# State product and decay transposes moved by one step each in a Mamba-2 branch beside large products

## The chip, the cores and the metric

The kernel runs on one core of one Trainium2 chip. The metric is the device time of one execution in microseconds (us). A core has TensorE (PE in the profile; PEld is its weight load), VectorE (DVE), ScalarE (ACT), GpSimd (POOL) and SyncE (SP, which here only issues transfers). PE writes its results to PSUM, in banks of 128 partitions by 512 32-bit numbers; DVE and ACT read them from there.

## The reference, cut to what matters

One decoder layer on 512 positions of width 1024: a norm, one large projection into all branches, three branches in parallel (dilated attention, causal pooling, Mamba-2 SSD), gates, a projection back, and a gated feed-forward with a convolution. The change lies in the SSD branch:

```python
def ssd_scan(x, dt, A, Bm, Cm):
    ...
    a = (dt * A).reshape(b, c, l, h).transpose(0, 3, 1, 2)
    a_cs = jnp.cumsum(a, axis=-1)
    ...
    Lmat = jnp.exp(jnp.where(causal, seg, -jnp.inf)).reshape(b, g, e, c, l, l)
    cb = jnp.einsum("bclgn,bcsgn->bcgls", Cc, Bc)
    y_diag = jnp.einsum("bcgls,bgecls,bcsgep->bclgep", cb, Lmat, xc)
    decay = jnp.exp(a_cs[..., -1:] - a_cs).reshape(b, g, e, c, l)
    states = jnp.einsum("bclgn,bgecl,bclgep->bcgepn", Bc, decay, xc)
    chunk_decay = jnp.exp(a_cs[..., -1]).reshape(b, g, e, c)

    def step(carry, inp):
        st, dec = inp
        return carry * dec[..., None, None] + st, carry
    ...
    out_decay = jnp.exp(a_cs).reshape(b, g, e, c, l)
    y_off = jnp.einsum("bclgn,bcgepn,bgecl->bclgep", Cc, prev, out_decay)
    return (y_diag + y_off).reshape(b, s, h, p)
```

There are 4 chunks of 128 positions and 2 groups of 8 heads. For each pair (chunk c, group gi): `y_diag` is a product with decays inside the chunk, `states` is what the chunk adds to the state, and `y_off` is what the state left by the chunks before contributes.

## The kernel before, in words

**The large products.** All weight products run in 32-bit numbers split into a high and a low part: three products (`mm3`, line 228, matmuls at line 234) replace one. Weights pass through a fixed pipeline: SP loads a block `raw` (line 183), ACT makes the high part `wh` (line 195), DVE the remainder `wl` (line 215), PE multiplies. A job is one such block; a 512-column result with 8 row blocks of weights takes 24 matmuls.

**Steps.** The smaller work of the branches stands between these products. Each such piece is a Python generator: `step()` (line 156), called after a result of the large products (in some jobs twice in one), takes the next waiting item into the running set and lets every running item advance to its next `yield`. A plain `yield` ends the item's part of this step. `yield ROWS`, `yield WHOLE` and `yield REST` postpone what follows to a later phase of the same step: first all items run up to such a mark, then all with `ROWS`, then `WHOLE`, then `REST`. So an item's place among the steps, and its phase, decide where its instructions stand in the queue of each engine. PE, ACT, DVE and POOL run in exactly the order written (line 106, `ORDERED`), each strictly in its queue's order; the semaphores between them are added by the framework from who reads and writes what.

**Buffers.** PSUM has 8 banks: 4 for the large products (`MM`) and 4 (`SM`, line 114) shared by all small pieces: score products `ps`, score transposes `pt`, value products `po`, and those of the SSD branch. A new small tile gets the bank that was given back first, and its first product waits for the last reader of the tile that held the bank. The 512-wide tiles in SBUF come from a common set of 54 (`T`, line 108) in the same way.

**The cumulated decays** (`ssd_prep`, line 834) run between the products of the pooling branch's output, beside the first group of attention heads. One step forms the cumulated decays as `pcs` (lines 873 and 874) and copies them to `acs`; the next step transposes them into `pact` (line 888). DVE copies `pact` (line 890), ACT takes its exponential (line 893), and SP stores both to DRAM (`ad`, line 892; `ed`, line 895). They are read back by transfers much later, in the scan (lines 920 and 926).

**The scan** (`ssd_start`, line 989) begins after the products of the branch's inputs and runs beside the third group of attention heads and the first gates. It puts one `ssd_item` for each (c, gi) on the waiting list in the order `SSD_ORDER` = (0,0), (1,0), (0,1), (2,0), (1,1), (3,0), (2,1), (3,1), with a free place after each; the attention's items take these free places. So a new item starts every second step, and an item takes five steps:

1. the loads of the decays (SP, lines 920 and 926), then in `WHOLE` the transposes of x (`pxs`, line 931), the product `pcb` (line 937), their readers on DVE (lines 933 and 939), and POOL's product with decays `xd` (line 942, not for c = 3)
2. the decays inside the chunk, DVE (line 948) and ACT (line 949)
3. their product with `pcb` on DVE (line 953)
4. for c of 1 and 2: POOL's product of the old state with the chunk's decay, into the new state `nw` (tile `st`, line 957)
5. `py` (line 963), and in `WHOLE`: for c > 0 the product `pyo` with the old state (line 970), DVE's product and sum with it (lines 972 and 973), the addition to the output (line 976); then, for c < 3, the state product `pst` (line 981), which is copied by ACT for c = 0 (line 984) and added to `nw` by DVE otherwise (line 986)

`prev[gi]` holds the group's last state. The next item of the same group reads it in its own steps 4 and 5.

Of the kernel before, what the change touches and what calls it, by code (L numbers as in the profile page):

```python
# [13 lines left out]
OP = mybir.AluOpType  # L14
AX = mybir.AxisListType

P = 128
# [66 lines left out]
def trunk(ctx: ExitStack, tc, out, x, rel_bias, ln1_g, w_in, b_gate, w_a, pool_w, pool_scale, w_b,  # L84
# [3 lines left out]
    act, dve, pool, pe, sp = nc.scalar, nc.vector, nc.gpsimd, nc.tensor, nc.sync  # L88
# [19 lines left out]
    def T(name, dt=F32, shape=(P, S)):  # L108
        return big.tile(list(shape), dt, name=name, tag="t")
# [4 lines left out]
    def SM(name):  # L114
        return psum.tile([P, S], F32, name=name, tag="sm")
# [32 lines left out]
    ROWS, WHOLE, REST = 1, 2, 3  # L148
# [664 lines left out]
    XS, YT, Y = {}, {}, {}  # L813
# [20 lines left out]
    def ssd_prep():  # L834

        f = lambda nme: cst.setdefault(nme, cpool.tile([P, n16], F32, name=nme))
        b16 = cpool.tile([P, 2, SH], F32, name="b16")
        for i, src in enumerate((ssd_dt_bias, ssd_a_log)):
            sp.dma_start(b16[:, i, :], src[0].partition_broadcast(P))

        dr, gr = T("dr"), T("gr")
        sp.dma_start(dr[:8, S - 2:], ssd_d[0].rearrange("(c h) -> c h", h=2))
        sp.dma_start(gr[:8, :P], ssd_norm_w[0].rearrange("(c p) -> c p", p=P))
        yield
        dve.tensor_copy(dr[:8, :P].rearrange("p (h d) -> p h d", h=2),
                        dr[:8, S - 2:].unsqueeze(2).to_broadcast([8, 2, DH]))
        dgc = cst["dgc"] = cpool.tile([P, 16], F32, name="dgc")
        v4 = lambda t: t.rearrange("p (a b) -> p a b", a=4)
        bc = lambda i: b16[:, i, :].unsqueeze(1).to_broadcast([P, 4, SH])
        xx, t, u, s, zz, dtv, a = (f(nme) for nme in ("dtx", "dtt", "dtu", "dts", "dtz", "dtv", "dta"))  # L850
        dve.tensor_tensor(v4(xx), dtr, bc(0), OP.add)
        dve.scalar_tensor_tensor(t, xx, -1.0, xx, OP.mult, OP.max)
        act.activation(t, t, AF.Exp, scale=-1.0)
        act.activation(b16[:, 1, :], b16[:, 1, :], AF.Exp)
        yield
        dve.tensor_scalar(u, t, 2.0, None, OP.add)
        dve.reciprocal(u, u)
        dve.tensor_mul(s, t, u)
        dve.tensor_mul(zz, s, s)
        dve.tensor_scalar(u, zz, 2.0 / 17, 2.0 / 15, OP.mult, OP.add)  # L860
        for d in (13, 11, 9, 7, 5, 3, 1):
            if d == 9:
                yield
            dve.tensor_mul(u, u, zz)
            dve.tensor_scalar(u, u, 2.0 / d, None, OP.add)
        dve.tensor_mul(u, u, s)
        dve.scalar_tensor_tensor(dtv, xx, 0.0, u, OP.max, OP.add)
        dve.scalar_tensor_tensor(v4(a), v4(dtv), -1.0, bc(1), OP.mult, OP.mult)
        yield
        yield  # L870
        yield WHOLE
        ps = SM("pcs")
        pe.matmul(ps[:, :n16], tri, a, start=True, stop=True)
        pe.matmul(ps[:, n16:2 * n16], ones, a, start=True, stop=True)
        for i, r in enumerate((dr, gr)):
            pe.transpose(ps[:, 2 * n16 + 8 * i:2 * n16 + 8 * i + 8], r[:8, :P], eye[:8, :8])
        dve.tensor_copy(dgc, ps[:, 2 * n16:2 * n16 + 16])
        acs, tot, dec = (f(nme) for nme in ("acs", "tot", "dec"))
        dve.tensor_copy(acs, ps[:, :n16])
        dve.tensor_copy(tot, ps[:, n16:2 * n16])  # L880
        dve.tensor_tensor(dec, tot, acs, OP.subtract)
        act.activation(dec, dec, AF.Exp)
        act.activation(tot, tot, AF.Exp)
        yield
        yield WHOLE
        pt = SM("pact")
        for c in range(4):
            pe.transpose(pt[:SH, c * P:(c + 1) * P], acs[:, c * SH:(c + 1) * SH], eye)
        at, et = T("acst"), T("east")
        dve.tensor_copy(at[:SH], pt[:SH])  # L890
        ad = cst["ad"] = dram.tile([SH, S], F32, name="ad")
        sp.dma_start(ad, at[:SH])
        act.activation(et[:SH], pt[:SH], AF.Exp)
        ed = cst["ed"] = dram.tile([SH, S], F32, name="ed")
        sp.dma_start(ed, et[:SH])

    def hb(t, c, h0, n=8):
        return t[:, c * SH + h0:c * SH + h0 + n].unsqueeze(2).to_broadcast([P, n, DH])

    def h3(t):  # L900
        return t.rearrange("p (h d) -> p h d", h=8)

    btok, prev, done = {}, {}, set()
# [9 lines left out]
    def ssd_item(c, gi):  # L913
        cs = slice(c * P, (c + 1) * P)
        dtv, acs, dec, tot, ad, ed = (cst[n] for n in ("dtv", "acs", "dec", "tot", "ad", "ed"))
        als = []
        for q in range(2):
            al = T("al")
            h0 = 8 * gi + 4 * q
            sp.dma_start(al.rearrange("p (h l) -> p h l", h=4), ad[h0:h0 + 4, cs].partition_broadcast(P))  # L920
            als.append(al)
        if c:
            ea = T("ea")
            for i in range(2):
                h0 = 8 * gi + i
                sp.dma_start(ea[DH * i:DH * i + DH].rearrange("p (j l) -> p j l", j=4),
                             ed[h0:h0 + 8 - i:2, cs].partition_broadcast(DH))
        yield WHOLE
        ps = SM("pxs")
        for j in range(4):  # L930
            pe.transpose(ps[:, j * P:(j + 1) * P], XS[4 * gi + j][:, cs], eye)
        xc = T("xc")
        dve.tensor_tensor(h3(xc), h3(ps), hb(dtv, c, 8 * gi), OP.mult)  # L933

        y = Y[gi][:, :, cs]
        pcb = SM("pcb")
        pe.matmul(pcb[:, :P], XS[8 + gi][:, cs], XS[10 + gi][:, cs], start=True, stop=True)
        cbt = T("cbt", F32, (P, P))
        dve.tensor_tensor(cbt, pcb[:, :P], tri, OP.mult)
        if c < 3:  # L940
            xd = T("xd")
            pool.tensor_tensor(h3(xd), h3(xc), hb(dec, c, 8 * gi), OP.mult)  # L942
        yield
        for q in range(2):
            a3 = als[q].rearrange("p (h l) -> p h l", h=4)
            for j in range(4):
                i = c * SH + 8 * gi + 4 * q + j
                dve.tensor_scalar(a3[:, j, :], a3[:, j, :], acs[:, i:i + 1], 0.0, OP.subtract, OP.min)
            act.activation(als[q], als[q], AF.Exp)
        yield  # L950
        for q in range(2):
            a3 = als[q].rearrange("p (h l) -> p h l", h=4)
            dve.tensor_tensor(a3, a3, cbt.unsqueeze(1).to_broadcast([P, 4, P]), OP.mult)
        yield
        if c and c < 3:
            nw = T("st")
            pool.tensor_tensor(h3(nw), h3(prev[gi]), hb(tot, c, 8 * gi), OP.mult)
        yield
        py = SM("py")
        for j in range(4):  # L960
            for i in range(2):
                o, lo = (2 * j + i) * DH, (2 * j + i) % 4 * P
                pe.matmul(py[DH * i:DH * i + DH, j * P:(j + 1) * P], xc[:, o:o + DH],  # L963
                          als[j // 2][:, lo:lo + P], start=True, stop=True)
        by_j = lambda t: t.rearrange("p (j l) -> p j l", j=4)
        yield WHOLE
        if c:
            po = SM("pyo")
            for j in range(4):
                pe.matmul(po[:, j * P:(j + 1) * P], prev[gi][:, j * P:(j + 1) * P], XS[10 + gi][:, cs],  # L970
                          start=True, stop=True)
            dve.tensor_tensor(ea, po, ea, OP.mult)
            dve.tensor_tensor(ea, ea, py, OP.add)
        for j in range(4):
            m = 4 * gi + j
            dve.scalar_tensor_tensor(y[:, j, :], y[:, j, :], cst["dgc"][:, m:m + 1],
                                     by_j(ea if c else py)[:, j, :], OP.mult, OP.add)
        done.add((c, gi))
        if c < 3:
            pst = SM("pst")  # L980
            pe.matmul(pst, btok[gi][:, cs], xd, start=True, stop=True)  # L981
            if c == 0:
                nw = T("st")
                act.copy(nw, pst)
            else:
                dve.tensor_tensor(nw, nw, pst, OP.add)
            prev[gi] = nw

    def ssd_start():
        for m in (8, 9, 0, 1, 2, 3, 10, 4, 5, 6, 7, 11):  # L990
# [366 lines left out]
    def program():  # L1357
# [4 lines left out]
        yield from pool_out_job()  # L1362
        yield Call(lambda: attend(0))
        yield Call(lambda: waiting.insert(3, ssd_prep()))
        for i, job in enumerate(branch_jobs(1, w_b, YB, 8, more=range(7))):
            if i == 3:
# [262 lines left out]
```

## Time and profile before

| what | value |
|---|---|
| three runs | 1044.83, 1042.64, 1044.0 us; median 1044.0 |
| the profiled execution | 1044.41 us, of which the span of the profile is 1042.1 |
| clock granted to PE in it, mean | 0.997 |
| instructions in the span | 13072 |
| state products `pst` (line 981) | 6, in two rows each, from 398.6 to 484.6 us of the span |
| transposes `pact` (line 888) | 4, at 163.5 us |

A row of the profile names the line, the engine, the operation and the tiles as out<-in. Matmuls overlap with those behind them and their ends are modelled, so distances from start to start tell more than durations. A product of plain 32-bit numbers shows as two rows. The idle time in square brackets counts from the modelled end of the engine's instruction before, and the arrow names what ended it.

### The profile page before, as it was taken

To read this page: it belongs to the slowest core of one execution; us is meant where nothing else is said; L and a number is where in the kernel's file an instruction comes from. 1 tells how busy PE (TensorE), PEld (TensorE's weight loads), DVE (VectorE), ACT (ScalarE), POOL (GpSimd) and SP (SyncE) were. 2 spreads that over 40 slices of the span, in tenths; PEclk is the share of its full clock that TensorE was granted. 3 is DMA by queue.
4 is the path that set the end of the run, shared out by engine and by line. 5 is a ranking of instruction groups with operands and counts; after the bars stand their busy time and mean duration, and the time that the engine had idled before them with its cause. 6 is when DMAs were issued, how large, how long until landed. Compare 5 with 4: busy or idle time off the path is not lost.

```text
span 1042.1 us, 13072 instructions
## 1 busy us (share of the span) xinstructions
PE 1028.6 (99%) x5196; PEld 859.2 (82%) x5196; DVE 688.9 (66%) x924; ACT 483.2 (46%) x779; POOL 136.9 (13%) x118
## 2 busy tenths in 40 slices
PE   8999999999999999999999999999999999999997
PEld 8988877898888887777888888898888888888885
DVE  4563556774356658666568755767778769876776
ACT  5432445443474363466555333544445544454332
POOL 1680000000000001100134500001111000111002
PEclk9999999999999999999999999999999999999999
DMA  8445222126322354542244535543222232412222
GB/s 272 128 109 155 88 75 75 31 56 186 102 81 81 81 151 112 142 130 53 81 139 136 181 102 202 165 142 121 82 94 69 81 122 84 159 41 81 81 81 81
DMA packets 116427, 115.51 MB, mean 111 GB/s; under 512 B 5235, under 2 KB 101302, under 8 KB 116367
## 3 DMA queue, kind: packets, MB, share of 16 engines
q1 hardware_dynamic: 115775, 113.83, 36.0%
q8 instruction: 41, 0.67, 0.3%
q10 hardware_dynamic: 592, 0.86, 0.2%
q14 instruction: 19, 0.16, 0.0%
HBM read 110.87 MB, written 2.22 MB: 109 GB/s over the span
## 4 chain that ended last, share of the span: by engine, by line
PE 96%; ACT 1%; DVE 1%; DMA 1%; issue 0%; ACTq 0%; DVEq 0%
PE pa L234 35%; PE pu L234 22%; PE pb L234 12%; PE pqk L234 9%; PE pd L234 7%; PE pa L1480 2%; PE pu L1290 1%; PE ps L661 1%; PE pt L690 1%; PE ppw L234 1%; PE po L702 1%; PE py L963 1%; DMA eye<-in_c_eye_dram 1%; PE uT L1497 1%; PE pyo L970 1%; PE pst L981 0%
## 5 line engine op out<-in xcount | busy, mean ns | idle before, releaser
L215 DVE TENSOR_TENSOR wl<-raw,wh 128x2048 fp32r<-128x2048 f32 (+3 forms) x92 | 213.3, 2318 | 53.1 <-ACT wh L195 44.5
L195 ACT CAST wh<-raw 128x1024 fp32r<-128x1024 f32 (+3 forms) x182 | 183.7, 1026 | 43.3 <-DMA raw<-in_w_in_dram 16.3
L234 PE MATMUL pa<-uh,wh 128*128 128x512 f32 x384 | 99.0, 400 | 0.0
L1163 DVE SCALAR_TENSOR_TENSOR hc<-pu,fcol,hc 128x510 f32<-128x510 f32 x88 | 65.8, 748 | 49.0 <-ACT hc L1160 47.4
L234 PE MATMUL pa<-ul,wh 128*128 128x512 f32 x384 | 95.0, 390 | 0.0
L234 PE MATMUL pa<-uh,wl 128*128 128x512 f32 x384 | 94.9, 389 | 0.0
L234 PEld LDWEIGHTS pa<-ul,wh 128*128 128x128 f32 x384 | 72.1, 188 | 15.2
L234 PEld LDWEIGHTS pa<-uh,wl 128*128 128x128 f32 x384 | 72.1, 188 | 14.9
L234 PE MATMUL pu<-uh,wh 128*128 128x512 f32 (+1 forms) x352 | 83.6, 380 | 0.0
L234 PE MATMUL pu<-uh,wl 128*128 128x512 f32 (+1 forms) x352 | 83.6, 380 | 0.0
L234 PE MATMUL pu<-ul,wh 128*128 128x512 f32 (+1 forms) x352 | 83.5, 380 | 0.0
L234 PEld LDWEIGHTS pa<-uh,wh 128*128 128x128 f32 x384 | 70.3, 188 | 15.2 <-issue 1.4
L234 PEld LDWEIGHTS pu<-uh,wl 128*128 128x128 f32 x352 | 64.2, 188 | 12.5
L234 PEld LDWEIGHTS pu<-ul,wh 128*128 128x128 f32 x352 | 64.2, 188 | 12.5
L234 PEld LDWEIGHTS pu<-uh,wh 128*128 128x128 f32 x352 | 64.1, 188 | 12.4
L1168 POOL TENSOR_TENSOR hc<-hc 128x512 f32<-128x512 f32 x22 | 31.7, 1442 | 288.6 <-DVE hc L1163 253.6
L1160 ACT ACTIVATE hc<-pu,fcol,fcol 128x512 f32<-128x512 f32 x40 | 31.2, 779 | 80.5 <-PE pu L234 80.5
L942 POOL TENSOR_TENSOR xd<-xc,dec 128x512 f32<-128x512 f32 x6 | 6.5, 1080 | 358.3 <-DVE xc L933 351.2
L683 ACT ACTIVATE sb<-sb,nm 128x128 f32<-128x128 f32 (+1 forms) x72 | 30.0, 419 | 29.2 <-DVE nm L680 16.5
L1061 ACT ACTIVATE sg<-pa,col 128x512 f32<-128x512 f32 x24 | 16.5, 687 | 55.3 <-PE pa L234 55.2
L234 PE MATMUL pqk<-uh,wh 128*128 128x512 f32 x144 | 36.9, 394 | 0.0
L234 PE MATMUL pqk<-ul,wh 128*128 128x512 f32 x144 | 36.3, 390 | 0.0
(347 smaller groups left out, 1817.4 us busy)
## 6 DMA issues: line engine op xcount, KB each, us to landing
raw<-in_w_in_dram SPq DMA_DIRECT2D x25, 1024.0 KB
raw<-in_ffn_w_up_dram SPq DMA_DIRECT2D x22, 1024.0 KB
raw<-in_w_in_dram SPq DMA_DIRECT2D x20, 512.0 KB
raw<-in_w_o_dram SPq DMA_DIRECT2D x8, 1024.0 KB
raw<-in_ffn_w_down_dram SPq DMA_DIRECT2D x6, 1024.0 KB
raw<-in_w_b_dram SPq DMA_DIRECT2D x4, 1024.0 KB
al<-ad SPq DMA_DIRECT2D x16, 256.0 KB
w<-in_ffn_w_down_dram SPq DMA_DIRECT2D x4, 1024.0 KB
```

Of the source, the lines that this page charges most:

```text
L195: act.copy(job.high[:, :, o], job.raw[:, :, o])
L215: (eng or dve).tensor_tensor(l[:, :, o], job.raw[:, :, o], h[:, :, o].bitcast(F32), OP.subtract)
L234: pe.matmul(ps, l, r, start=first and n == 0, stop=last and n == total - 1)
L661: pe.matmul(pss[i][:, o:o + w * P], q[r, n * P:(n + 1) * P], k[r, kb * P:(kb + w) * P], start=True, stop=True)
L683: act.activation(sb[:, off:off + w * P], sb[:, off:off + w * P], AF.Exp, bias=nm[:, n, h:h + 1], accum_out=ls[:, n, h:h + 1])
L690: pe.transpose(pt[:, o:o + P], sb[:, o:o + P], eye)
L702: pe.matmul(po[DH * hh:DH * hh + DH, n * P:(n + 1) * P], V[g, kb + i][:, (2 * c + hh) * DH:(2 * c + hh + 1) * DH], probs[2 * c + hh, nb][: ...
L1061: act.activation(s, ps, AF.Sigmoid, bias=col[:, o:o + 1])
L1160: act.activation(t, ps, AF.Identity, bias=ff["c1"][:, ff["b"] + m:ff["b"] + m + 1], scale=fw(2, m))
L1163: dve.scalar_tensor_tensor(t[:, sh:], ps[:, :S - sh], fw(k, m), t[:, sh:], OP.mult, OP.add)
L1168: pool.tensor_tensor(a, a, t, OP.mult)
L1480: pe.matmul(first[2 * n + j][:, lo:hi], a[:, k, j * P:(j + 1) * P], b[:, k, lo:hi], start=a is wh and b is uh and k == 0, stop=a is wl and ...
```

## The change

In `ssd_prep` one more plain `yield` puts the transposes `pact`, their two readers and the two stores one step later. In `ssd_item` the state product and its copy or addition move from the end of step 5 into step 4: the product into the phase `WHOLE`, the copy or addition into `REST`. POOL's product with the decay stays ahead of them in step 4. Since the new state is now made before step 5 reads the old one, step 5 uses the old state under the name `old`. The number of instructions of each kind stays the same.

```diff
@@ ssd_prep
         act.activation(dec, dec, AF.Exp)
         act.activation(tot, tot, AF.Exp)
         yield
+        yield
         yield WHOLE
         pt = SM("pact")
         for c in range(4):
@@ ssd_item
             dve.tensor_tensor(a3, a3, cbt.unsqueeze(1).to_broadcast([P, 4, P]), OP.mult)
         yield
-        if c and c < 3:
+        old = prev.get(gi)
+        if c < 3:
             nw = T("st")
-            pool.tensor_tensor(h3(nw), h3(prev[gi]), hb(tot, c, 8 * gi), OP.mult)
+            if c:
+                pool.tensor_tensor(h3(nw), h3(old), hb(tot, c, 8 * gi), OP.mult)
+            yield WHOLE
+            pst = SM("pst")
+            pe.matmul(pst, btok[gi][:, cs], xd, start=True, stop=True)
+            yield REST
+            if c == 0:
+                act.copy(nw, pst)
+            else:
+                dve.tensor_tensor(nw, nw, pst, OP.add)
+            prev[gi] = nw
         yield
         py = SM("py")
@@
         if c:
             po = SM("pyo")
             for j in range(4):
-                pe.matmul(po[:, j * P:(j + 1) * P], prev[gi][:, j * P:(j + 1) * P], XS[10 + gi][:, cs],
+                pe.matmul(po[:, j * P:(j + 1) * P], old[:, j * P:(j + 1) * P], XS[10 + gi][:, cs],
                           start=True, stop=True)
@@
         done.add((c, gi))
-        if c < 3:
-            pst = SM("pst")
-            pe.matmul(pst, btok[gi][:, cs], xd, start=True, stop=True)
-            if c == 0:
-                nw = T("st")
-                act.copy(nw, pst)
-            else:
-                dve.tensor_tensor(nw, nw, pst, OP.add)
-            prev[gi] = nw
```

## The prediction

> **What bounds the kernel now.** I read the page first: busy shares, then the chain that ended last.
>
> ```profile
> span 1042.1 us, 13072 instructions
> ...
> PE 1028.6 (99%) x5196; PEld 859.2 (82%) x5196; DVE 688.9 (66%) x924; ACT 483.2 (46%) x779; POOL 136.9 (13%) x118
> ...
> PE 96%; ACT 1%; DVE 1%; DMA 1%; issue 0%; ACTq 0%; DVEq 0%
> ```
>
> PE is the bound: 99% busy and 96% of the chain. A change that issues the same products can only gain where PE stands still. So I cut the span into the stretch with the cumulated decays (124 to 195 us), the one with the scan (371 to 515) and what follows up to the last stage (515 to 991); the columns are length, then the busy time of PE, PEld, DVE, ACT and POOL, then the granted clock, DMA share and GB/s.
>
> ```profile
> 124.00:195.00 71.00, 69.61 (x413) 54.56 (x412) 44.45 (x96) 36.78 (x87) 0.00 (x0) 1.00 0.22 68
> 371.00:515.00 144.00, 142.94 (x836) 114.68 (x835) 94.86 (x182) 82.70 (x142) 14.66 (x12) 1.00 0.43 114
> 515.00:991.00 476.00, 475.93 (x2209) 397.42 (x2208) 349.13 (x385) 217.73 (x298) 71.32 (x47) 1.00 0.35 114
> ```
>
> PE idles 71.00 - 69.61 = 1.39 us in the first, 1.06 in the second, 0.07 in the third. What was saved earlier is not eaten by an idle PE in the third; its work simply moves forward. The clock is 1.00 in all three, so there is nothing to win or lose there. PE's waits, grouped, say who ends these pauses:
>
> ```profile
> PE pt L690 <- ACT east L893: 1.4, 1, 1.4
> ...
> PE pst L981 <- DVE ea L972: 0.9, 1, 0.9
> ```
>
> Both are waits for one of the four small PSUM banks (the tiles of `SM`), and both stand at instructions that the change moves.
>
> **Part 1, the transposes of the cumulated decays (L888) one step later.** The timeline, columns start, duration, instruction, idle time before it:
>
> ```profile
> 163.49 0.60 PE L888 MATMUL pact<-eye,acs 128*16 128x128 f32 x4
> 164.13 0.68 DVE L890 COPY acst<-pact 16x512 f32<-16x512 f32 x1 [3.72 <-PE pact L888]
> 164.83 0.33 SPq L892 DMA_DIRECT2D ad<-acst  x1
> 164.84 0.59 ACT L893 ACTIVATE east<-pact 16x512 f32<-16x512 f32 x1 [1.81 <-DVE acst L890]
> 165.48 0.55 PE L690 MATMUL pt<-eye,sb 128*128 128x128 f32 x3 [1.39 <-ACT east L893]
> ```
>
> The score transposes `pt` that follow at once get the bank of `pact` itself, so they wait until DVE and then ACT have read it. Four transposes take 0.43 us from start to start (pxs 419.60 to pcb 420.04 in a fence below), so `pt` could have begun at 163.49 + 0.43 = 163.92 and began at 165.48: 1.56 us lost; the row's 1.39 counts from a modelled end.
>
> In the built program of the changed kernel `pt` stands alone in the first of the two steps and waits for no reader; `pact` comes 12 products later, with the next head's `pt` right behind it. That `pt` waits for the score addition (DVE L676) of the first score tile and for its own exponentials, no longer for L893. These readers are ready: after the earlier `pt`, DVE has a copy and that addition to do, 0.56 and 0.68 us in the rows at 166.13 and 166.61, against 2.77 us of products before `pact` is due (twelve products in the chain of waits, below at 166.03).
>
> ```profile
> 166.13 0.56 DVE L691 COPY sb<-pt 128x384 f32<-128x384 f32 x1 [1.33 <-PE pt L690]
> 166.61 0.68 DVE L676 TENSOR_TENSOR sb<-ps,b 128x512 f32<-128x512 f32 x1
> ...
> 169.22 0.48 ACT L691 COPY sb<-pt 128x384 f32<-128x384 f32 x1
> ...
> 171.81 0.88 PE L702 MATMUL po<-sb,v 128*64 128x128 f32 x12
> ```
>
> ```profile
> 166.03 2.77 PE pa L234 x12
> ...
> 485.24 5.49 PE pa L234 x24
> ```
>
> So 1.56 us go. What is late next: ACT now has L893 (0.59) ahead of the copy L691 that the value product `po` needs. That copy ended at 169.70, 2.1 us ahead of `po` at 171.81; with 0.59 more ahead of it, about 1.5 remain, still cover. Without the cover it would cost at most 0.59. The two stores behind L890 and L893 move along on SP:
>
> ```profile
> 165.59 0.33 SPq L895 DMA_DIRECT2D ed<-east  x1
> 178.20 11.69 SPq L183 DMA_DIRECT2D raw<-in_w_in_dram  x2
> ...
> 385.88 1.13 SPq L920 DMA_DIRECT2D al<-ad  x2
> ```
>
> One step (3 us) later they still leave SP about 9 us ahead of the next weight load, and their first reader comes at 385.88. Cost nothing. Part 1: -1.56, between -0.97 (cover gone) and -1.6.
>
> **Part 2, the state product (L981) and the state's addition one step sooner.** Nothing is added: six products, two copies (L984), four additions (L986), four POOL products (L957), as before. Two places lose time now. The first:
>
> ```profile
> 482.11 1.16 PE L970 MATMUL pyo<-xcv,st 128*128 128x128 f32 x8
> 483.30 0.69 DVE L972 TENSOR_TENSOR ea<-pyo,ea 128x512 f32<-128x512 f32 x1 [3.21 <-PE pyo L970]
> ...
> 484.14 1.10 PE L981 MATMUL pst<-xd,btok 128*128 128x512 f32 x2 [0.88 <-DVE ea L972]
> ```
>
> `pst` takes the bank of `pyo` and waits for L972. Undisturbed, the next instruction follows 0.99 us after `pyo` begins (433.61 to 434.60 below); here 484.14 - 482.11 = 2.03. Lost: 1.04. In the new order weight products follow `pyo` here and no small tile is wanted for another 5.49 us (the 24 products at 485.24 in the chain), so all of it goes. The second:
>
> ```profile
> 433.61 1.16 PE L970 MATMUL pyo<-xcv,st 128*128 128x128 f32 x8
> 434.60 1.02 PE L981 MATMUL pst<-xd,btok 128*128 128x512 f32 x2
> 434.80 0.69 DVE L972 TENSOR_TENSOR ea<-pyo,ea 128x512 f32<-128x512 f32 x1 [2.97 <-PE pyo L970]
> ...
> 435.55 0.66 PE L931 MATMUL pxs<-eye,xs 128*128 128x128 f32 x4
> 436.27 0.49 PE L937 MATMUL pcb<-xcv 128*128 128x128 f32 x2
> ```
>
> Free of waits, `pxs` would start at 434.60 + 0.86 = 435.46 and `pcb` 0.43 later, 435.89; it starts at 436.27, so 0.38 is lost now. Without `pst` in between, `pxs` starts at 434.60, `pcb` is due at 435.03, and in the built program `pcb` there takes `pyo`'s bank: it waits for L972, that is until about 435.55. Lost then: 0.52. The wait grows by 0.14, because `pst` was part of its cover.
>
> Price of the moved product itself: it took 0.86 after `pyo` and 0.96 after `py`:
>
> ```profile
> 407.82 1.02 PE L981 MATMUL pst<-xd,btok 128*128 128x512 f32 x2
> 408.68 0.60 PE L931 MATMUL pxs<-eye,xs 128*128 128x128 f32 x4
> ...
> 418.64 1.12 PE L981 MATMUL pst<-xd,btok 128*128 128x512 f32 x2
> 419.60 0.60 PE L931 MATMUL pxs<-eye,xs 128*128 128x128 f32 x4
> 420.04 0.39 PE L937 MATMUL pcb<-xcv 128*128 128x128 f32 x2
> ```
>
> No row has it between weight products. Bounds: 0.10 less for the two that stood behind `py`, 0.10 more for the four that stood behind `pyo`: -0.2 to +0.4. I take 0: a weight product is full width like `pyo`, the row it is nearest to, which says 0.86 again, and I do not count the little that the other two might save.
>
> The addition L986 now follows the POOL product of the same step; durations from these rows (min/median/max ns):
>
> ```profile
> L957 POOL TENSOR_TENSOR st<-st,tot x4: 1035/1043/1045, 403.5 to 466.5; 128x512 f32<-128x512 f32 x4
> L986 DVE TENSOR_TENSOR st<-st,pst x4: 673/680/687, 410.5 to 485.8; 128x512 f32<-128x512 f32 x4
> ```
>
> The tightest is the step at 403: POOL runs its product from 403.53 to 404.56, DVE gets to the addition at 405.55, where L953 stands now, 1 us later. Behind L986 in DVE's queue are L953, the score additions L676 and the weight remainders L215. Those L953 results feed the `py` just ahead of the `pst` at 418.64, over 10 us on; 0.68 us more ahead of them is covered. If all four waited a whole POOL product the queue would be 1.7 us late each time, still inside that cover. Cost 0.
>
> ```profile
> 403.53 1.03 POOL L957 TENSOR_TENSOR st<-st,tot 128x512 f32<-128x512 f32 x1
> ...
> 405.55 1.47 DVE L953 TENSOR_TENSOR al<-al,cbt 128x512 f32<-128x512 f32 x2
> ```
>
> **Sum.** -1.56 - 1.04 + 0.14 = -2.46. The profiled execution took 1044.41 us (2.3 around its span); that gives 1041.95, say 1042.0. The median of the three runs is 1044.0, 0.4 lower, and would give 1041.5; the runs scatter from 1042.64 to 1044.83, so I keep 1042.0.
>
> **The rivals.**
> *The bank wait moves on (10%).* With the same four banks, `pst` now takes one in steps that also hold two score tiles; the second place shows how one wait feeds the next. If the 1.04 comes back at another small tile, -1.56 + 0.14 is left: 1043.0. For it: the 0.14. Against it: in the built program every other small tile there waits for a reader that stands in its queue well ahead of PE. The Trainium skill (Perfetto Trace Analysis, Optimization Strategy) says that repeated bubbles can mean too little PSUM for the next tile; by that rule this rival would be the likely one. The trace shows two pauses in six such steps and not a repeated one, which speaks for the first sum.
>
> *The transposes' wait goes with them (6%).* If `pt` behind `pact` still waited for L893, the change would not do what it says in part 1: -1.04 + 0.14, 1043.5. For it: `pact` and a `pt` stand next to each other again. Against it: the wait in the built program names other readers.
>
> *Slower: weight loads come into the open (7%).* Each state product has two loads, and the weight product behind it one:
>
> ```profile
> L981 PEld LDWEIGHTS pst<-xd,btok x12: 186/192/193, 398.6 to 484.2; 128*128 128x128 f32 x12
> ```
>
> If none hid behind the long products now around it, 3 x 0.19 x 6 = 3.4 us come on top: -2.46 + 3.4 = +0.9, 1045.4. It decides from 0.41 us for each product. For it: 32-bit products between those of the weights have no row. Against: at 418.64 the same loads are hidden (0.96 in all). The Trainium skill (TensorE: Matmul & The Clock Gate, LDWEIGHTS) has a load's time follow from its columns, 107 ns for 128; by that estimate even full exposure, 1.9 us, would not undo the gain. The row has 192, and the row decides.
>
> *A better schedule behind it (3%).* DVE's queue gets shorter at the end of an item, which could also take the 0.52 at `pcb`: 1041.4.
>
> **How the numbers follow.** The forecast has 74%, the rivals 26. About 0.2% (2.1 us) is what a measurement can tell from no change; the forecast lies just beyond it. Its bounds, -0.97 - 1.04 + 0.14 + 0.4 = -1.5 and -1.6 - 1.04 + 0.14 - 0.2 = -2.7, put some 10 of its 74 points within 0.2%. Faster: 64 + 3 = 67%; same: 10 + 10 + 6 = 26%; slower: 7%. The range takes the bounds, the first and the last rival, and some 0.7 of scatter (two thirds of half of 2.2): from 1041.4 down to 1040.6 and from 1043.0 up to 1043.7.
>
> **What would show it.** PE's waits no longer list `pt` on L893 nor `pst` on L972; idle PE in the first stretch falls to about 0, in the second `pcb` near 433 waits 0.5 us for L972. The six `pst` take 0.86 to 0.96 to the next start. I am wrong if `pst` or its followers show pauses of 0.4 us, if the pause near 483 turns up at another small tile, or if weight products wait for L215.

## The result, and the profile after

| | changed kernel | kernel before, beside it |
|---|---|---|
| first measurement, median | 1039.74 us (1039.29 to 1041.28, 6 runs) | 1043.82 us (1042.24 to 1044.83, 6 runs) |
| ratio, 95% interval | 0.9966 [0.9953, 0.9979] | |
| profiled execution | 1041.28 us, span 1039.3 | 1044.41 us, span 1042.1 |

The change makes the kernel faster, and by the medians by more than the sum said: the median lies 2.3 us under the forecast of 1042.0 and 0.9 us under the low end of the range. The profiled execution of the changed kernel, 1041.28 us, the longest of its six, lies inside it. So two questions have to be kept apart: did the instructions do what was forecast, and where does the rest of the time come from?

The page of the changed kernel, in its own words (span, busy time of each engine, chain that ended last):

```profile
span 1039.3 us, 13067 instructions
...
PE 1028.4 (99%) x5196; PEld 859.6 (83%) x5196; DVE 689.2 (66%) x924; ACT 483.3 (47%) x779; POOL 136.4 (13%) x118
...
PE 97%; ACT 1%; DVE 1%; DMA 1%; issue 0%; ACTq 0%; DVEq 0%
```

PE is still the bound, with the same busy time to 0.2 us. The same three stretches of the changed kernel (columns as before: length, PE, PEld, DVE, ACT, POOL, clock, DMA share, GB/s):

```profile
124.00:195.00 71.00, 71.00 (x419) 55.89 (x418) 45.99 (x100) 37.58 (x88) 0.00 (x0) 1.00 0.22 68
371.00:515.00 144.00, 143.53 (x840) 115.47 (x839) 95.76 (x185) 80.80 (x140) 14.68 (x12) 1.00 0.43 114
515.00:991.00 476.00, 475.93 (x2209) 397.45 (x2208) 349.33 (x383) 220.57 (x302) 71.00 (x48) 1.00 0.35 114
```

PE's idle time in the first stretch is gone, in the second 0.47 us is left, in the third nothing moved. PE's waits of the changed kernel, whole list:

```profile
PE uT L1500 <- DVE v L1506: 1.9, 1, 1.9
PE pa L1441 <- DVE relb L515: 1.1, 1, 1.1
PE pcb L938 <- DVE ea L984: 0.3, 1, 0.3
PE pb L234 <- DVE wl L215: 0.3, 1, 0.3
```

The two waits that the prediction named, `pt` on L893 and `pst` on L972, are not there; `pcb` on the pyo product's reader is new, as forecast. The places themselves, in the timeline of the changed kernel (lines from 886 on stand one to three, in `ssd_item` up to twelve, lower in the file than before, and `pst` is L963 now):

```profile
166.33 0.60 PE L889 MATMUL pact<-eye,acs 128*16 128x128 f32 x4
...
166.77 0.49 PE L690 MATMUL pt<-eye,sb 128*128 128x128 f32 x3
...
167.68 0.59 ACT L894 ACTIVATE east<-pact 16x512 f32<-16x512 f32 x1 [0.84 <-DVE acst L891]
...
168.18 0.45 ACT L691 COPY sb<-pt 128x384 f32<-128x384 f32 x1
...
169.94 0.88 PE L702 MATMUL po<-sb,v 128*64 128x128 f32 x12
...
432.67 1.16 PE L982 MATMUL pyo<-xcv,st 128*128 128x128 f32 x8
...
433.67 0.60 PE L932 MATMUL pxs<-eye,xs 128*128 128x128 f32 x4
433.87 0.69 DVE L984 TENSOR_TENSOR ea<-pyo,ea 128x512 f32<-128x512 f32 x1 [2.08 <-PE pyo L982]
...
434.61 0.49 PE L938 MATMUL pcb<-xcv 128*128 128x128 f32 x2 [0.34 <-DVE ea L984]
...
481.35 1.16 PE L982 MATMUL pyo<-xcv,st 128*128 128x128 f32 x8
482.27 2.09 PE L234 MATMUL pa<-uh,wh 128*128 128x512 f32 x8
```

`pt` starts 0.44 us after `pact`, as four transposes take; it does not wait for L894, which runs 0.9 us later. The copy L691 ends at 168.63, 1.3 us ahead of `po` at 169.94: its cover held. Behind `pyo` at 481.35 the weight products come after 0.92 us; before, it was 2.03 to `pst`. And `pcb` starts 0.94 us after `pxs` where 0.43 is free of waits: 0.51 lost, forecast 0.52.

Now the whole. Each execution is cut at PE's first weight product (L1480, in the changed kernel L1483) and at its last (`pb`). Of the kernel before and of the changed kernel, timeline rows of the first products and of the last pair:

```profile
14.12 0.72 PE L1480 MATMUL pa<-uh,wh 128*128 128x256 f32 x4
...
1034.51 0.61 PE L234 MATMUL pb<-wl,fh 128*128 128x512 f32 x2
```

```profile
13.82 0.72 PE L1483 MATMUL pa<-uh,wh 128*128 128x256 f32 x4
...
1031.75 0.61 PE L234 MATMUL pb<-wl,fh 128*128 128x512 f32 x2
```

From the first product to the last pair: 1034.51 - 14.12 = 1020.39 before, 1031.75 - 13.82 = 1017.93 after. The difference is 2.46 us, and the sum of the prediction was -2.46. The other 0.30 of the span came from an earlier first product, and some 0.3 more from what lies around the span (1044.41 - 1042.1 = 2.3 before, 2.0 after). The same cut of all profiled executions (starts of the first and of the last single product, 0.23 us behind the pair's; from there to the end it is 7.37 or 7.38 us in each):

| kernel | first product at | first to last product | profiled time |
|---|---|---|---|
| before | 14.12 | 1020.62 | 1044.41 |
| changed | 13.82 | 1018.16 | 1041.28 |
| e1: before again | 15.13 | 1020.58 | 1045.24 |
| e2: changed again | 13.96 | 1018.14 | 1041.39 |
| e3: part 1 alone | 12.17 | 1019.06 | 1040.96 |
| e4: part 2 alone | 14.27 | 1019.71 | 1043.33 |
| e5: exponentials from the copy | 13.71 | 1021.02 | 1044.65 |
| e6: x transposes sooner | 11.84 | 1018.54 | 1039.89 |
| e7: `pcb` later | 13.60 | 1017.36 | 1040.46 |
| e8: longer warm-up | 12.22 | 1018.13 | 1039.82 |
| e9: e7 and e8 | 12.35 | 1017.90 | 1039.64 |

The third column repeats to 0.04 us where a kernel was profiled twice. The second spreads over 3.3 us, and by 1.0 us between two executions of the kernel before. That is where a median of six runs can come out 2 us from where the instructions would put it.

### The profile page after: what moved, and what is told of

Read it like the earlier page. It is cut to its first block, busy times and chain, and to the rows that moved or that the text cites. A ratio compares the mean times of both kernels' runs of the same rounds, so it can differ in the third digit from the quotient of the medians.

```text
span 1039.3 us, 13067 instructions
## 1 busy us (share of the span) xinstructions
PE 1028.4 (99%) x5196; PEld 859.6 (83%) x5196; DVE 689.2 (66%) x924; ACT 483.3 (47%) x779; POOL 136.4 (13%) x118
## 4 chain that ended last, share of the span: by engine, by line
PE 97%; ACT 1%; DVE 1%; DMA 1%; issue 0%; ACTq 0%; DVEq 0%
PE pa L234 35%; PE pu L234 22%; PE pb L234 12%; PE pqk L234 9%; PE pd L234 7%; PE pa L1483 2%; PE pu L1293 1%; PE ps L661 1%; PE pt L690 1%; PE ppw L234 1%; PE po L702 1%; PE py L975 1%; DMA eye<-in_c_eye_dram 1%; PE uT L1500 1%; PE pyo L982 1%; PE pst L963 1%
```

## The experiments

**e1 and e2: both kernels again, unchanged.** There is no edit.

> The kernel before, unchanged, against itself. Theory A (the change is worth the 2.46 us by which PE's products moved together in the two traces, and the rest of the 4.1 us between the medians is scatter from one execution to the next that sits ahead of the first product): the ratio holds 1.000, executions scatter by about 2 us, and in the trace the stretch from the first product to the last stays at 1020.6 us while the stretch ahead of it differs. Rival B (all of the 4.1 us belongs to the change): the ratio also holds 1.000, but the scatter of single executions stays well under 2 us.

> The changed kernel once more, on the same chip as the runs beside it. Theory A: 0.9976 of before (2.46 us less), first product to last product 1018.2 us in the trace. Rival B: 0.9961 (4.1 us less), with a gain in some stretch that the first pair of traces did not show.

The kernel before, run as if it were a new one: 1042.59 us (1042.36 to 1045.24, 11 runs) beside 1043.87 (1041.94 to 1045.63, 31 runs), ratio 0.9995 [0.9986, 1.0004]. Two medians of one kernel differ by 1.3 us, while the interval of the ratio holds 1. The changed kernel: 1041.38 us (1040.22 to 1042.86, 9 runs), ratio 0.9975 [0.9965, 0.9985], that is -2.6 us. The forecast against its own base, 1041.95 / 1044.41 = 0.9976, lies in this interval and in the first one; the 0.9961 that e2's rival named lies outside. So the kernel is some 2.5 us faster, and the first measurement's 1039.74 was a set of mostly short runs. Four of those six have spans of 1037.3 to 1038.1 us; they have no trace, but an estimate with 1018.16 and 7.37 us held fixed puts their first products at 11.8 to 12.6 us, about as early as in e3 and e6. Their mean granted clocks, 0.998 or 0.999 against 0.996 and 0.997 in the other two, fit that.

**e3 and e4: each part alone.** e3 is the kernel before with the one added `yield`, e4 the kernel before with the changed `ssd_item`.

```diff
@@ e3, ssd_prep
         yield
+        yield
         yield WHOLE
         pt = SM("pact")
```

```diff
@@ e4, ssd_item
-        if c and c < 3:
+        old = prev.get(gi)
+        if c < 3:
             nw = T("st")
...
+            yield WHOLE
+            pst = SM("pst")
+            pe.matmul(pst, btok[gi][:, cs], xd, start=True, stop=True)
+            yield REST
```

> Only the decay transposes one step later; the state product stays in step 5. Theory A: 1.56 to 1.66 us less, ratio 0.9985; first product to last 1019.0; PE no longer waits for L893 but still about 1.0 us before the state product near 482. Rival (the wait goes along with the transposes): no gain, 1.000.

> Only the state product, its copy and its addition one step sooner; the decay transposes stay. Theory A: 1.04 - 0.14 = 0.90 us less, ratio 0.9991; first product to last 1019.7; PE still waits 1.4 us for L893 at 165. Rival (the bank wait moves to another small tile): 0.14 us more, 1.000.

From first to last product e3 takes 1019.06 us, 1020.62 - 1019.06 = 1.56 less than before (forecast 1.56); e4 takes 1019.71, 0.91 less (forecast 1.04 - 0.14 = 0.90). Together they make 2.47, and both at once made 2.46: the parts are independent. The times: e3 1042.29 us (1040.96 to 1043.91, 11 runs), ratio 0.9988 [0.9979, 0.9997]; e4 1042.78 us (1040.95 to 1043.8, 11 runs), 0.9985 [0.9976, 0.9994]. Neither interval could have told 0.91 from 1.56; the traces could. The row of PE's waits that is left in e3 at these tiles, then those of e4:

```profile
PE pst L982 <- DVE ea L973: 0.9, 1, 0.9
```

```profile
PE pt L690 <- ACT east L893: 1.4, 1, 1.4
...
PE pcb L937 <- DVE ea L983: 0.3, 1, 0.3
```

Each part removes its own wait and leaves the other; the wait of `pcb` belongs to part 2.

**e5: is it the bank?** One execution of the kernel before, with ACT's exponential L893 reading the copy that DVE had just made, so that the last reader of `pact`'s bank is DVE, 0.6 us sooner.

```diff
-        act.activation(et[:SH], pt[:SH], AF.Exp)
+        act.activation(et[:SH], at[:SH], AF.Exp)
```

> The kernel before, with the exponential of the cumulated decays (L893) taken from their copy in SBUF instead of from the PSUM tile; nothing else moves. Theory A (the score transposes behind them wait for the last reader of the bank): that reader is now DVE's copy L890, so PE waits for L890 and starts the transposes some 0.6 us sooner; about 0.8 us of wait in the row, first product to last 1020.0 instead of 1020.6. Rival (they wait for ACT for another reason, such as its place in the queue): still 1.4 us on L893, 1020.6.

Timeline of e5 around the transposes, and a row of PE's waits that the kernel before doesn't have:

```profile
163.08 0.60 PE L888 MATMUL pact<-eye,acs 128*16 128x128 f32 x4
...
164.46 0.55 PE L690 MATMUL pt<-eye,sb 128*128 128x128 f32 x3 [0.77 <-DVE acst L890]
```

```profile
PE pu L234 <- ACT uh L452: 0.7, 1, 0.7
```

`pt` now waits for the copy instead of the exponential and starts 1.38 us after `pact` (before: 165.48 - 163.49 = 1.99), 0.61 sooner. It is the bank's last reader that PE waits for, on ACT in the kernel before and on DVE here. The time from first to last product did not fall, though: a new wait in the feed-forward, at 696 us, took it back. It comes from a weight transfer that landed late in this execution; e9 shows the same, and it is read there.

**e6: can the wait of `pcb` be moved away by taking the small tiles sooner?** One execution of the changed kernel, with `pxs` and `pcb` in the phase `ROWS` ahead of `pyo`.

```diff
-        yield WHOLE
+        yield ROWS
         ps = SM("pxs")
```

> The changed kernel with the new item's transposes pxs and product pcb put into the phase ROWS, so that they stand ahead of the older item's pyo. If the pause of pcb on pyo's bank (0.5 us in the changed kernel) could simply be stepped over, first to last product falls from 1018.2 to about 1017.6. Rival (the four banks are short there, and the wait passes to pyo, which then needs the bank that the same step's DVE work has to free): a pause of 0.7 to 0.9 us at pyo or pcb, 1018.6.

PE's waits of e6:

```profile
PE pcb L938 <- ACT o L708: 0.6, 1, 0.6
PE pyo L982 <- DVE xc L934: 0.6, 1, 0.6
```

From first to last product it takes 1018.54 us, 0.38 more than the changed kernel. The wait on L984 is gone and two others stand in its place, for two other readers: with four banks in turn, moving a tile sooner handed the wait to the tiles that now come behind it.

**e7: and by taking them later?** The changed kernel, with the product `pcb` and its copy moved from step 1 to step 2, phase `WHOLE`, where their result is still in time for step 3.

```diff
@@ step 1
-        pcb = SM("pcb")
-        pe.matmul(pcb[:, :P], XS[8 + gi][:, cs], XS[10 + gi][:, cs], start=True, stop=True)
-        cbt = T("cbt", F32, (P, P))
-        dve.tensor_tensor(cbt, pcb[:, :P], tri, OP.mult)
@@ step 2, behind the exponentials
+        yield WHOLE
+        pcb = SM("pcb")
+        pe.matmul(pcb[:, :P], XS[8 + gi][:, cs], XS[10 + gi][:, cs], start=True, stop=True)
+        cbt = T("cbt", F32, (P, P))
+        dve.tensor_tensor(cbt, pcb[:, :P], tri, OP.mult)
         yield
```

> The changed kernel with the product pcb and its masked copy one step later (step 2, phase WHOLE), so that a step that starts an item wants one small bank less. Theory A: the waits of pcb near 434 (0.52) and 466 (0.25) go and no other comes; 0.8 us less than the changed kernel, first product to last 1017.4, ratio to before 0.9968. Rival (the wait moves on to another small tile, or the later masked copy holds up py): no gain, 1018.2, 0.9976.

PE's waits of e7, whole list:

```profile
PE uT L1501 <- DVE v L1507: 1.9, 1, 1.9
PE pa L1442 <- DVE relb L515: 1.1, 1, 1.1
PE pb L234 <- DVE wl L215: 0.3, 1, 0.3
```

No wait for a small bank is long enough for this list any more, and first to last product takes 1017.36 us, 0.80 less than in the changed kernel. That is more than the 0.51 of the wait near 433 us. Most of the other 0.3 stands one item further on, as the expectation says. The changed kernel there, and then e7:

```profile
465.86 0.66 PE L932 MATMUL pxs<-eye,xs 128*128 128x128 f32 x4
466.54 0.49 PE L938 MATMUL pcb<-xcv 128*128 128x128 f32 x2
```

```profile
465.18 0.42 PEld L932 LDWEIGHTS pxs<-eye,xs 128*128 128x128 f32 x4 [0.31 <-ACT o L708]
```

In the changed kernel `pcb` follows `pxs` by 0.68 us here, 0.24 or 0.25 more than the row free of waits, and the kernel before had the same 0.68 (467.48 to 468.16). In e7 it is gone: 0.51 + 0.25 = 0.76 of the 0.80. What e7 leaves is a wait of `pxs` itself, some 0.3 us for ACT's L708, which the changed kernel has too. The time: 1040.52 us (1038.86 to 1041.64, 8 runs) beside 1042.96 (1041.96 to 1045.7, 16 runs), ratio 0.9976 [0.9965, 0.9986].

**e8: where do the 3 us of scatter come from?** The first rows of the spans differ between executions above all in the granted clock. Windows of the kernel before, then of e3, which happened to start early (columns as above, the clock is third from the end):

```profile
8.00:10.00 2.00, 1.46 (x7) 1.46 (x8) 1.38 (x7) 1.25 (x4) 0.00 (x0) 0.67 1.16 311
10.00:12.00 2.00, 2.00 (x11) 1.93 (x10) 0.07 (x1) 0.99 (x1) 1.94 (x1) 0.50 1.09 348
```

```profile
8.00:10.00 2.00, 1.77 (x15) 1.77 (x16) 1.28 (x7) 1.30 (x4) 0.25 (x1) 1.00 1.16 310
10.00:12.00 2.00, 2.00 (x18) 1.86 (x17) 0.55 (x2) 1.84 (x3) 2.00 (x1) 1.00 1.09 349
```

PE runs 12 warm-up products (`WARM`), then stands still until DVE has the norm's factors (L1503), then transposes x (`uT`, L1497). The first 16 transposes in the timelines of the kernel before and of e3:

```profile
8.54 3.69 PE L1497 MATMUL uT<-diag,xin 128*128 128x128 f32 x16 [2.55 <-DVE v L1503]
```

```profile
8.23 2.05 PE L1498 MATMUL uT<-diag,xin 128*128 128x128 f32 x16 [1.69 <-DVE v L1504]
```

3.69 us against 2.05 for the same products. With the clock at 0.50 they take longer, and the first weight product, which needs them, starts at 14.12 instead of 12.17. Theory: the pause ahead of the transposes lets the clock drop, and whether it does differs from execution to execution. In windows of 0.1 us the low stretch begins between 7.6 and 9.7 us and lasts 3.4 us in six of the seven executions that have one, and 6.8 us in e1. From the start of the transposes to the first weight product it is 3.94 or 3.95 us in the four executions without it, 5.48 to 5.58 in the six, and 6.70 in e1. So a low stretch costs 1.5 us, and the double one of e1 2.8; what is left of the 3.3 us of spread is when DVE has the factors, for the transposes start between 7.90 and 8.79 us. e8 fills the pause: the changed kernel with six more warm-up products.

```diff
-WARM = 12
+WARM = 18
```

> The changed kernel with 18 instead of 12 warm-up products, which fill part of PE's pause ahead of the first transposes. Theory A (the scatter from one execution to the next is the granted clock between 8 and 14 us, which falls to 0.50 in the executions in which that pause is long): the granted clock stays near 1.00 there, the first weight product comes at about 11.4 us after the first load's issue instead of 13.1 to 14.4, the executions scatter by less than 1 us, and the median falls to about 1039.7; first to last product stays 1018.2. Rival (the scatter comes from the loads' landing): the same scatter of 2 us or more around 1041.4.

A window of e8, and its first transposes:

```profile
8.00:10.00 2.00, 1.72 (x15) 1.72 (x16) 1.33 (x7) 1.38 (x5) 0.20 (x1) 1.00 1.17 308
```

```profile
8.28 2.05 PE L1500 MATMUL uT<-diag,xin 128*128 128x128 f32 x16 [0.30 <-DVE v L1506]
```

The pause is 0.30 us, the clock stays at 1.00 (in the windows from 8 to 14 us), the first product starts at 12.22, and first to last product is unchanged (1018.13). Nine runs lie between 1039.41 and 1040.44 us, 1.0 apart, where the nine of the changed kernel in e2 were 2.6 apart; median 1039.82, ratio 0.9965 [0.9955, 0.9975]. The median is that of the changed kernel's first six runs, 1039.74: four of those had, by the estimate under e2, started early by themselves. For 67 executions of the kernel before, beside e1 to e9, the mean granted clock is known, and it sorts their times: 28 at 0.999 took 1041.94 to 1043.22 us, 21 at 0.997 took 1043.55 to 1044.62, and eight at 0.994 or 0.995 took 1045.12 to 1045.70; the ten at 0.996 and 0.998 lie from 1042.17 to 1044.59. The rival, that the landing of the loads makes the scatter, is left with the 0.9 us at the start of the transposes.

**e9: both.** The changed kernel with the edits of e7 and e8.

> The changed kernel with both edits at once: pcb and its copy moved into the second step, and 18 warm-up products instead of 12. If the two are independent (the theory: one shortens the stretch between the weight products, the other the stretch ahead of them): first to last weight product 1017.36 us as in e7_pcb_later, first weight product at about 11.5 us as in e8_warm18, so about 0.8 us less than e8_warm18 in the profiled execution (1039.0 us), a ratio to the kernel before of about 0.9957, and times within some 1.1 us of each other. Rival: the late start was filled with waiting that the moved product also shortens, so the gains overlap: no further gain over e8_warm18, first to last product above 1017.9 us.

1039.26 us (1038.87 to 1039.64, 5 runs) beside 1043.84 (1042.12 to 1044.62, 9 runs), ratio 0.996 [0.9946, 0.9973]: the lowest median of all kernels here, 0.56 us under e8, though the intervals of e8 and e9 overlap. The first product starts at 12.35 (11.61 us behind the first transfer's issue, as expected), but first to last product takes 1017.90 in the profiled execution, not 1017.36. The trace says that neither theory holds as it was put. Against e7, the weight products of e9 keep their distances until 692 us and lose 0.54 there, all at one place. Timeline of e7, then of e9:

```profile
683.69 5.40 SPq L183 DMA_DIRECT2D raw<-in_ffn_w_up_dram  x2
...
688.96 1.99 ACT L195 CAST wh<-raw 128x1024 fp32r<-128x1024 f32 x2 [4.43 <-DMA raw<-in_ffn_w_up_dram]
```

```profile
682.42 5.40 SPq L183 DMA_DIRECT2D raw<-in_ffn_w_up_dram  x2
...
688.97 1.99 ACT L195 CAST wh<-raw 128x1024 fp32r<-128x1024 f32 x2 [5.72 <-DMA raw<-in_ffn_w_up_dram]
...
690.87 1.06 ACT L452 CAST uh<-uT 128x512 fp32r<-128x512 f32 x2
...
691.50 1.23 PE L234 MATMUL pu<-uh,wh 128*128 128x256 f32 x8 [0.28 <-ACT uh L452]
```

From SP's issue to ACT's cast it is 5.27 us in e7 and 6.55 in e9. ACT's copy L452 is queued behind that cast, and PE needs it. In nine of the eleven profiled executions this distance is 5.08 to 6.03 us and PE waits for nothing there; in e9 (6.55) and e5 (6.98) it does. So e5's and e9's third columns hold 1.0 and 0.5 us of a late transfer. Whether it lands late by chance or because e9 asks for it sooner is open: e6 and e8 ask at nearly the same time (683.06 and 683.08) and see 6.03 and 5.21.

## Why the prediction was right about the kernel and wrong about the time

**The bound and the three stretches** were read rightly. Idle PE went from 1.39 to 0 and from 1.06 to 0.47, the third stretch kept its 475.93, and the gain was carried to the end.

**Part 1**: -1.56 forecast, -1.56 in e3. What is late next was named too; the cover for L691 is 1.3 us instead of the 1.5 forecast.

**Part 2**: -0.90 forecast, -0.91 in e4. At `pcb` 0.51 is lost (0.52 forecast; the 0.43 in it is 0.44 by the printed rows, 420.04 - 419.60, which changes nothing). The moved product was taken at no price because a weight product is as wide as `pyo`. The chain of waits of the changed kernel has such a product between weight products:

```profile
390.32 2.75 PE pqk L234 x12
393.07 0.86 PE pst L963 x2
393.93 2.09 PE pqk L234 x9
```

0.86 us again, so the row it was taken from stands, and the rival with the weight loads in the open (from 0.41 us a product) does not happen. That the sum hits to 0.01 is partly luck. By the distances of the weight products in the two traces, the six products cost 5.18 us at their new places and, waits taken out, gave back 5.33 at the old ones: 0.15 that the sum put at nothing. Steps too small to place, most of them between 380 and 480 us, took about as much back.

**The other rivals.** The bank wait did not move on in the changed kernel, but e6 shows that it can, at the same four banks with another order. `pt` did not keep its wait. The better schedule, which would also take the 0.52 at `pcb`, does not come by itself; e7 had to write it. The prediction counted two places that lose time in part 2; there is a third, near 467 us of the kernel before, where `pxs` comes 0.27 and `pcb` 0.25 late. The change leaves it as it was, so the sum is not touched, but "two pauses in six such steps" speaks less clearly against the first rival than it was taken to.

**The step that failed** is the last one, in the words of the prediction: "some 0.7 of scatter (two thirds of half of 2.2)", on a forecast made from one execution's 1044.41 ("the runs scatter from 1042.64 to 1044.83, so I keep 1042.0"). It took the scatter for noise around a middle, small for a median. (By its own term the low end would be 1041.4 - 0.7 = 1040.7 and not 1040.6; either way the median lies below it.) The runs showed a start-up that is early or late, mostly by the granted clock (1.5 to 2.8 us, e8): the first weight product starts anywhere from 11.84 to 15.13 us. Put around the changed kernel's fixed part, with 1.9 to 2.5 us around the span as these executions have it, this gives 11.84 + 1018.16 + 7.37 + 1.9 = 1039.3 to 15.13 + 1018.16 + 7.37 + 2.5 = 1043.2. The 15 runs of the changed kernel in the first measurement and e2 lie from 1039.29 to 1042.86. A median of a few runs can fall on nearly any part of that, and the range should have started near 1039.5. The profiled execution of before, used as base, was a late starter (14.12), with 0.67 and 0.50 of clock in its windows, and its transposes took 5.58 us to the first product instead of 3.94. Without that, 1044.41 - 2.46 - 1.64 = 1040.3, an estimate; the 0.6 from there to 1039.74 is of the size by which the start of the transposes (0.9) and the time around the span (0.6) differ. In the prediction the statement "the clock is 1.00 in all three" was true and left out the start-up, the one stretch ahead of the last product in which these windows show it lower.

The Trainium skill (TensorE: Matmul & The Clock Gate, What's actually happening) has a clock gate that halves the clock after an idle window of about 3.4 us, in windows that run free of the kernel's start, so that the same kernel meets it differently from run to run. The halves, 0.50 and 1.00, and the change from run to run agree with the rows, and so does the length of the low stretches, 3.4 us and once 6.8. The length of the pause doesn't: the pauses ahead of the transposes were 1.88 to 2.95 us long in the seven executions whose clock fell to 0.50, and 0.30 to 1.69 in the four in which it stayed at 1.00. Nor was the stretch ahead of the drop idle: in the 3.4 us before it PE was busy for 0.9 to 1.5 us. How little PE may do there without losing the clock, these runs do not settle.

## What to carry to other kernels

Where a change is worth less than the scatter of the runs, compare two traces between two instructions that both kernels share, here the first and the last large product: that repeated to 0.04 us while executions differed by 3. It is not proof against a transfer that lands late in between (1.0 us in e5, 0.5 in e9), so read where the distance was lost before putting it down to the change. Before a range is drawn around a sum, look in the trace of before for what differs between executions, the start-up and its clock first, and give the range that width. In this kernel a small tile that PE must wait for is waiting for the last reader of its bank, so the cure is an order in which no reader is still queued when the bank's turn comes, and each such move is to be read for the tile that gets the bank next.

## What was not expected of the hardware

The granted clock fell to 0.50 after pauses of PE of only 1.88 us (e7: 0.80 in the window from 8 to 10 us and 0.50 from 10 to 12), and stayed at 1.00 after one of 1.69 (e3). First weight products then start at 13.60 to 15.13 us instead of 11.84 to 12.35, so a pause at the start decides over 1.5 to 2.8 us, about as much as the whole change brings; six warm-up products more, in a pause that had nothing else to do, took away both the cost and most of the scatter. And the same 1 MB weight load took between 5.08 and 6.98 us from its issue to its first reader, at a place where PE has cover for about 6.
